# Cross-attention with its query and output weights folded into K and V, and norm chains that run on into the next stage

## The chip, the cores and the metric

One Trainium2 chip, 8 cores. Each core computes one of the eight batch elements with the same program and the same weights. The metric is the device time of the slowest core in microseconds. Some executions fall in a slow state, in which the cores of one die show a lower granted clock and the time is 3% to 16% longer; they are left out of every comparison here, for the kernel before and for every other.

Names of engines in the profile: PE is TensorE's matmuls, PEld its weight loads, DVE is VectorE, ACT ScalarE, POOL GpSimd, SP the queue that issues the large transfers. An *eviction* is the copy of a finished matmul group from PSUM into its buffer in SBUF. A line of a timeline gives start and length in us, engine, line of the kernel, operation, out<-in, shapes and count, and in brackets how long the engine stood idle before it and what ended that.

## The reference

Two layers, each FFN, token mixer, cross-attention, FFN, every part between two RMS norms. Only the attention matters here:

```python
def cross_attention(h, m, wq, wkv, wo):          # h (B, 2048, 1024), m (B, 256, 1024)
    q = (h @ wq).reshape(b, s, XA_HEADS, XA_HEAD_DIM)       # 4 heads of 256
    k, v = jnp.split(m @ wkv, 2, axis=-1)                   # 256 memory tokens
    scores = jnp.einsum("bshd,bmhd->bhsm", q, k) * (XA_HEAD_DIM ** -0.5)
    p = jax.nn.softmax(scores, axis=-1)
    o = jnp.einsum("bhsm,bmhd->bshd", p, v).reshape(b, s, D_MODEL)
    return o @ wo
# around it:
    m = rms_norm(mem, mem_norm_g[l])
    h = cross_attention(rms_norm(x, g[4]), m, xa_wq[l], xa_wkv[l], xa_wo[l])
    x = x + rms_norm(h, g[5])
```

With 256 memory tokens and heads of 256, Wq K and V Wo of a head are as large as K and V themselves, so the products may be taken in another order.

## The kernel before

Activations lie transposed, channels on the 128 partitions, the 2048 positions in four blocks of 512 ("tb"). X is the residual stream (f32), XN its normed copy (bf16), HO the output of a sub-layer before its post-norm. Weights stream from HBM as panels of 128 x 1024 into eight slots; GpSimd issues them in its own order, among its additions.

The kernel is written as a list of operations per engine, and norm work is put between matmul groups by *deferred steps*: a step has a count, every matmul group outside a step is one tick, and a step whose count has run out is emitted. A step is also forced out at once if an operation needs what it still has to write, or would overwrite what it still has to read (`_check`). The chain of a finished half (post-norm, residual add, pre-norm of the next sub-layer) is a sequence of such steps. Before the change, queueing a new sequence empties the old one on the spot:

```python
        def run_seq(steps):
            while any(d[1] == ("seq",) for d in k.deferred):
                k.need(("seq",))                 # flush of the old chain
            ...
# HalfOut.finish: the chain of two blocks ta, tb_ after the second half
                steps = [(2, fin_stats)] + [(1, A(ta, c0)) for c0 in cs]      # A: HO *= r; X += HO
                ...
                    steps += [(1, both(A(tb_, 0), sa0)), (1, A(tb_, 1)), (1, A(tb_, 2)), (1, both(A(tb_, 3), sb0)),
                              (1, A(tb_, 4)), (1, A(tb_, 5)), (1, both(A(tb_, 6), sc10)), (1, both(A(tb_, 7), sc20)),
                              (2, sa1), (3, sb1), (3, sc11), (1, sc21)]
                run_seq(steps)
```

`sa` squares four of the eight channel tiles on ScalarE, `sb_` sums them on TensorE and squares the others, `sc1` sums those, takes the reciprocal root and writes half of XN, `sc2` the rest.

Attention before, in order (cut):

```python
            for hf, c8 in [(0, c_) for c_ in range(8)]:      # Q of blocks 0, 1; memory norm among it
                w = ws.acquire(("lin", "xa_wq", l, c8))
                ...
            for hf, c8 in [(1, c_) for c_ in range(4)]: ...   # Q of blocks 2, 3, half
            for c8 in range(8): ...                           # K
            for cb in range(4): ...                           # V
            for hf, c8 in [(1, c_) for c_ in range(4, 8)]: ...
            for sb_ in range(NTB):
                for h in range(4): ...                        # scores, exp; then sum, P V, O = . / sum
            out_proj(lambda c: [("lin", "xa_wo", l, c)], rhs, 8, l, n_post, False, nxt, ho2=...)
```

The softmax here doesn't subtract the row's maximum and nothing guards it: scores larger than these inputs give would overflow.

Of the kernel before, what the change touches and what calls it, by code (L numbers as in the profile page):

```python
# [96 lines left out]
def panel_specs():  # L97
    specs = []
    for l in range(L):
        for f in range(2):  # L100
            for j in range(NJ):
                for nm, gu in (("ffn_w_gate", "g"), ("ffn_w_up", "u")):
                    specs.append((("gu", l, f, j, gu), 1024,
                                  lambda inp, c, nm=nm, l=l, f=f, j=j: _pkc(inp[nm][l, f][:, j * 128:(j + 1) * 128])))
            for c in range(8):
                for pc, (r0, r1) in enumerate(((0, 1024), (1024, 2048), (2048, 2816))):
                    specs.append((("d", l, f, c, pc), (r1 - r0),
                                  lambda inp, cc, l=l, f=f, c=c, r0=r0, r1=r1:
                                  _pkc(inp["ffn_w_down"][l, f][r0:r1, c * 128:(c + 1) * 128])))
        for nm, ncol in (("xa_wq", 8), ("xa_wkv", 8), ("xa_wo", 8)):  # L110
            for c in range(ncol):
                specs.append((("lin", nm, l, c), 1024,
                              lambda inp, cc, nm=nm, l=l, c=c: _pkc(inp[nm][l][:, c * 128:(c + 1) * 128])))
        for cb in range(4):
            for kh in range(2):
                specs.append((("wv", l, cb, kh), 1024,
                              lambda inp, cc, l=l, cb=cb, kh=kh:
                              _pkc(inp["xa_wkv"][l][kh * 512:(kh + 1) * 512, 1024 + cb * 256:1024 + (cb + 1) * 256])))
# [57 lines left out]
class K:  # L176
    ENGS = ("pe", "act", "dve", "pool", "sp")

    def __init__(self, sched=None):
# [5 lines left out]
        self._in_def = False  # L185
        self._bank = 0
# [137 lines left out]
    def _tick(self):  # L324
        if self._in_def:
            return
        for d in self.deferred:
            d[0] -= 1
# [115 lines left out]
def build(nsub=8):  # L444
# [50 lines left out]
    O = AT(nc, "O", 0, [8, S], BF16)  # L495
    HO2 = AT(nc, "HO2", 32768, [8, 1024], F32)
    Q = AT(nc, "Q", 32768, [8, S], BF16)
    M32 = AT(nc, "M32", 65536, [8, MEM], F32)
    MN = AT(nc, "MN", 73728, [8, MEM], BF16)
    KT = AT(nc, "KT", 65536, [8, MEM], BF16)  # L500
    V = AT(nc, "V", 69632, [2, D], BF16)
    ET = [AT(nc, "ET%d" % i, 86016 + i * 2048, [2, TB], BF16) for i in range(3)]
    RD = [AT(nc, "RD%d" % i, 92160 + i * 2048, [TB], F32) for i in range(2)]
# [8 lines left out]
    def program(k):  # L512
# [40 lines left out]
        def run_seq(steps):  # L553
# [9 lines left out]
            def go(i):  # L563
# [4 lines left out]
                def wrapped():  # L568
                    fn()
                    go(i + 1)  # L570
                if d <= 0:
# [64 lines left out]
        class HalfOut:  # L636
# [34 lines left out]
            def finish(self, nxt, hf, cpb=1):  # L671
# [76 lines left out]
                run_seq(steps)  # L748
# [15 lines left out]
        def out_proj(pkeys_for_c, rhs, nk, l, n_post, half, nxt, ho2=None):  # L764
            for hf in range(2):
                tbs = (2 * hf, 2 * hf + 1)
                held = []
                ho = HalfOut(l, n_post, half, tbs, hoap=(ho2 if hf == 1 else None))
# [27 lines left out]
        def ffn(l, f, n_post, nxt):  # L796
            for hf in range(2):
# [3 lines left out]
                for j in range(NJ):  # L801
                    wg = ws.acquire(("gu", l, f, j, "g"))
# [377 lines left out]

        def attention(l, n_post, nxt):
            for tb in range(NTB):
                need_xn(tb)
            m32, m32k = M32((0, 8), (0, MEM))
            k.dma("sp", lambda e: e.dma_start(out=m32, in_=memT.rearrange("(c p) m -> p c m", p=128)), "ml", writes=m32k)
            mst = {"pend": [], "mb": None, "gi": 0}

            def mem_sq(c):
                map_, mk = M32(c, (0, MEM))
                i = k.rot("SQD", 3)  # L1190
                k.op("act", lambda e: e.activation(out=SQD[i][:, 0:MEM], in_=map_, func=AF.Square),
                     reads=mk, writes=[("SQD", i)])
                mst["pend"].append((c, i))

            def mem_mm():
                c, i = mst["pend"].pop(0)
                if mst["mb"] is None:
                    mst["mb"] = k.bank(reserve=True)
                mb = mst["mb"]
                k.mm(P[mb][:, 0:MEM], [(ONESM[:, :], SQD[i][:, 0:MEM], [("SQD", i), ("ONES",)])], mb,  # L1200
                     start=(c == 0), stop=(c == 7))

            def mem_apply():
                r = rstd_from(mst["mb"], MEM, 1.0)
                for c in range(8):
                    map_, mk = M32(c, (0, MEM))
                    oap, okeys = MN(c, (0, MEM))
                    col = CF[:, CF_MG + l * 8 + c:CF_MG + l * 8 + c + 1]
                    k.op("dve", lambda e, map_=map_, oap=oap, col=col: e.scalar_tensor_tensor(
                        out=oap, in0=map_, scalar=col, in1=R[r][:, 0:MEM], op0=ALU.mult, op1=ALU.mult),  # L1210
                        reads=mk + [("R", r)] + CONST, writes=okeys)
            for hf, c8 in [(0, c_) for c_ in range(8)]:
                w = ws.acquire(("lin", "xa_wq", l, c8))
                for tb in (2 * hf, 2 * hf + 1):
                    lo, hi = tbr(tb)
                    b = k.bank()
                    k.mm(P[b][:, :], [(w.w(kk),) + tuple(_rk(XN(kk, (lo, hi)), w.key)) for kk in range(8)], b)
                    oap, okeys = Q(c8, (lo, hi))
                    evac_copy(oap, okeys, b, eng="act")
                    gi = mst["gi"]  # L1220
                    mst["gi"] += 1
                    if 6 <= gi < 14:
                        mem_mm()
                    if 4 <= gi < 12:
                        mem_sq(gi - 4)
                    if gi == 14:
                        mem_apply()
                ws.release(w)
            for hf, c8 in [(1, c_) for c_ in range(4)]:
                w = ws.acquire(("lin", "xa_wq", l, c8))  # L1230
                for tb in (2 * hf, 2 * hf + 1):
                    lo, hi = tbr(tb)
                    b = k.bank()
                    k.mm(P[b][:, :], [(w.w(kk),) + tuple(_rk(XN(kk, (lo, hi)), w.key)) for kk in range(8)], b)
                    oap, okeys = Q(c8, (lo, hi))
                    evac_copy(oap, okeys, b)
                ws.release(w)
            for c8 in range(8):
                w = ws.acquire(("lin", "xa_wkv", l, c8))
                b = k.bank()  # L1240
                k.mm(P[b][:, 0:MEM], [(w.w(kk),) + tuple(_rk(MN(kk, (0, MEM)), w.key)) for kk in range(8)], b)
                oap, okeys = KT(c8, (0, MEM))
                evac_copy(oap, okeys, b, n=MEM, eng="act")
                ws.release(w)
            for cb in range(4):
                wv0 = ws.acquire(("wv", l, cb, 0))
                wv1 = ws.acquire(("wv", l, cb, 1))
                for mt in range(2):
                    b = k.bank()
                    pairs = []  # L1250
                    for kk in range(8):
                        map_, mk = MN(kk, (mt * 128, (mt + 1) * 128))
                        sl = wv0 if kk < 4 else wv1
                        pairs.append((map_, sl.t[:, (kk % 4) * 256:(kk % 4 + 1) * 256], mk + [sl.key]))
                    k.mm(P[b][:, 0:256], pairs, b)
                    oap, okeys = V(mt, (cb * 256, (cb + 1) * 256))
                    evac_copy(oap, okeys, b, n=256)
                ws.release(wv0)
                ws.release(wv1)
            for hf, c8 in [(1, c_) for c_ in range(4, 8)]:  # L1260
                w = ws.acquire(("lin", "xa_wq", l, c8))
                for tb in (2 * hf, 2 * hf + 1):
                    lo, hi = tbr(tb)
                    b = k.bank()
                    k.mm(P[b][:, :], [(w.w(kk),) + tuple(_rk(XN(kk, (lo, hi)), w.key)) for kk in range(8)], b)
                    oap, okeys = Q(c8, (lo, hi))
                    evac_copy(oap, okeys, b)
                ws.release(w)
            for sb_ in range(NTB):
                lo, hi = tbr(sb_)  # L1270
                for h in range(4):
                    et = ET[k.rot("ET", 3)]
                    for mt in range(2):
                        b = k.bank()
                        pairs = []
                        for dc in range(2):
                            kap, kk_ = KT(2 * h + dc, (mt * 128, (mt + 1) * 128))
                            qap, qk = Q(2 * h + dc, (lo, hi))
                            pairs.append((kap, qap, kk_ + qk))
                        k.mm(P[b][:, :], pairs, b)  # L1280
                        eap, ek = et(mt, (0, TB))
                        k.op("act", lambda e, b=b, eap=eap: e.activation(out=eap, in_=P[b][:, :], func=AF.Exp, scale=1.0 / 16.0),  # L1282
# [120 lines left out]
```

## Time and profile before

| | before |
|---|---|
| time, fast runs | 2968.9 to 2972.2 us, median 2970.4 |
| matmuls (weight loads) | 12574 |
| TensorE busy, VectorE, ScalarE, GpSimd | 93%, 35%, 33%, 21% |
| one attention, mixer end to FFN start | 280 us (layer 0), 276 us (layer 1) |
| of that lost by TensorE | 62 and 61 us |

A matmul's record lasts 0.38 us, though dense 512-column matmuls start every 0.216 us; so busy time overlaps and hides lost time. The weight loads, one per matmul, times the dense pace give the time that a stretch would need; the rest of the stretch is lost, to waits or to the half clock. The lines are shown in the prediction, whose "Trace Analysis" is the Trainium skill's page "Perfetto Trace Analysis".

### The profile page before, as it was taken

The numbers are of one execution on the slowest core, as the hardware profiler recorded it, in microseconds if no ns is written. First come the engines' busy times: TensorE is split into PE (matmuls) and PEld (weight loads), VectorE is DVE, ScalarE is ACT, GpSimd is POOL, SyncE is SP. The second block draws the span as 40 slices with busy tenths as digits, with TensorE's granted clock in tenths as the row PEclk, the third lists the DMA queues.
The fourth block names the chain that finished last, engine by engine and source line by source line (L and its number), as shares of the span: only waits on it lengthen the run. The fifth ranks groups of instructions, "written<-read, shape, count | busy, mean of one in ns | idle before, by whom it ended". The sixth has DMA issues, their size and how long they took to land.

```text
span 2968.9 us, 36707 instructions; the slowest of 8 cores (2963.8 to 2968.9 us)
## 1 busy us (share of the span) xinstructions
PE 2748.3 (93%) x12329; PEld 1231.4 (41%) x12574; DVE 1028.5 (35%) x1362; ACT 990.6 (33%) x1481; POOL 627.0 (21%) x915
## 2 busy tenths in 40 slices
PE   6999999976889899999999999979997898999996
PEld 2444444432334344444444444433443443444443
DVE  3211410774453451051052042135537236213212
ACT  4213312434636631241241242121146365113112
POOL 1113311221230221141121141120013113111121
PEclk9999999987999999999999999988999998999998
DMA  7554554523343345455455445431143523545567
GB/s 171 75 72 74 78 69 83 79 44 57 64 68 58 47 71 77 69 79 75 69 79 76 71 77 76 73 51 29 33 72 54 86 36 58 78 71 107 104 93 145
DMA packets 125510, 218.55 MB, mean 74 GB/s; under 512 B 14352, under 2 KB 29968, under 8 KB 125328
## 3 DMA queue, kind: packets, MB, share of 16 engines
q0 software_dynamic: 108432, 192.70, 43.6%
q1 hardware_dynamic: 16896, 23.48, 2.6%
q8 instruction: 107, 1.75, 0.2%
q14 instruction: 75, 0.61, 0.1%
HBM read 396.19 MB, written 8.39 MB: 136 GB/s over the span
## 4 chain that ended last, share of the span: by engine, by line
PE 82%; DVE 8%; ACT 5%; issue 3%; DMA 2%; POOL 0%; DVEq 0%; ACTq 0%; POOLq 0%; SPq 0%
PE ps L288 82%; DVE HO L695 3%; DVE XN L606 1%; DMA slot<-wflat 1%; DVE X L697 1%; ACT sqp L600 1%; ACT RD L1294 0%; ACT ET L1282 0%; DVE FE L919 0%; ACT r L538 0%; ACT RD L1295 0%; DVE ET L919 0%; DMA X<-xT 0%; ACT sqp L593 0%; ACT L538 0%
## 5 line engine op out<-in xcount | busy, mean ns | idle before, releaser
L288 PE MATMUL ps<-XN,slot 128*128 128x512 bf16 x7152 | 1621.7, 384 | 64.4 <-DVE XN L606 39.3
L288 PEld LDWEIGHTS ps<-XN,slot 128*128 128x128 bf16 x7296 | 718.6, 99 | 957.5 <-issue 123.6
L389 POOL DMA_DIRECT2D slot<-wflat x752 | 399.6, 536 | 2107.5 <-PE ps L288 2053.7
L823 DVE TENSOR_TENSOR H<-ps,s 128x512 bf16<-128x512 f32 x352 | 241.6, 689 | 1116.2 <-PE ps L288 1091.5
L288 PE MATMUL ps<-H,slot 128*128 128x512 bf16 x2756 | 622.4, 379 | 4.2 <-DMA slot<-wflat 1.1
L814 ACT ACTIVATE s<-ps 128x512 f32<-128x512 f32 x352 | 209.0, 597 | 801.8 <-PE ps L288 731.9
L288 PEld LDWEIGHTS ps<-H,slot 128*128 128x128 bf16 x2816 | 275.2, 98 | 334.6 <-issue 3.5
L652 ACT ACTIVATE HO<-ps,cf_sb 128x512 f32<-128x512 f32 x256 | 176.0, 688 | 535.5 <-PE ps L288 512.8
L695 DVE TENSOR_TENSOR HO<-HO,r 128x512 f32<-128x512 f32 x192 | 201.7, 1078 | 262.1 <-ACT r L540 262.1
L606 DVE SCALAR_TENSOR_TENSOR XN<-X,cf_sb,r 128x512 bf16<-128x512 f32 x256 | 176.7, 758 | 142.5 <-ACT r L540 142.5
L697 POOL TENSOR_TENSOR X<-X,HO 128x512 f32<-128x512 f32 x104 | 154.9, 1516 | 102.9 <-DVE HO L695 93.1
L655 ACT ACTIVATE sqd<-ps 128x512 bf16<-128x512 f32 x256 | 152.1, 594 | 58.7 <-PE ps L288 58.7
L288 PE MATMUL ps<-sqp,onesm 128*128 128x512 bf16 x251 | 78.6, 442 | 61.6 <-ACT sqp L593 33.8
L288 PE MATMUL ps<-O,slot 128*128 128x512 bf16 x500 | 117.7, 379 | 0.8
L288 PE MATMUL ps<-sqd,onesm 128*128 128x512 bf16 (+1 forms) x269 | 97.4, 378 | 13.1 <-ACT sqd L655 12.7
L733 DVE TENSOR_TENSOR HO<-HO,r 128x512 f32<-128x512 f32 x64 | 44.7, 732 | 140.0 <-ACT r L540 140.0
L600 ACT ACTIVATE sqp<-X 128x2048 bf16<-128x2048 f32 x32 | 61.1, 1909 | 62.8 <-PE ps L288 42.7
L288 PEld LDWEIGHTS ps<-O,slot 128*128 128x128 bf16 x512 | 49.9, 98 | 60.7 <-issue 1.1
L697 DVE TENSOR_TENSOR X<-X,HO 128x512 f32<-128x512 f32 x88 | 65.3, 742 | 9.5 <-DVE HO L695 0.5
L288 PEld LDWEIGHTS ps<-sqp,onesm 128*128 128x128 bf16 x256 | 25.6, 106 | 101.2 <-issue 81.3
L1141 ACT ACTIVATE s<-ps 128x512 f32<-128x512 f32 x32 | 19.1, 596 | 141.0 <-PE ps L288 115.0
L593 ACT ACTIVATE sqp<-X 128x2048 bf16<-128x2048 f32 x32 | 60.9, 1904 | 12.2 <-POOL X L697 12.2
(100 smaller groups left out, 1245.5 us busy)
## 6 DMA issues: line engine op xcount, KB each, us to landing
slot<-wflat POOLq DMA_DIRECT2D x680, 256.0 KB, 4.7
slot<-wflat POOLq DMA_DIRECT2D x72, 192.0 KB, 4.3
X<-xT SPq DMA_DIRECT2D x8, 1024.0 KB, 25.3
yT<-X SPq DMA_DIRECT2D x4, 2048.0 KB, 12.1
CP<-CR SPq DMA_DIRECT2D x64, 32.0 KB, 2.8
YB<-YP SPq DMA_DIRECT2D x64, 32.0 KB, 1.8
M<-memT SPq DMA_DIRECT2D x2, 1024.0 KB, 13.1
WT<-wt SPq DMA_DIRECT2D x1, 288.0 KB, 5.0
```

Of the source, the lines that this page charges most:

```text
L288: fn = (lambda e, l_=l_, r_=r_, st=st, sp=sp: e.matmul(out, lhsT=l_, rhs=r_, start=st, stop=sp))
L389: self.k.dma("pool", lambda e, dst=dst, src=src: e.dma_start(out=dst, in_=src), "w%d" % idx, reads=([("X", c, 0) for c in range(4)] if i = ...
L593: k.op("act", lambda e: e.activation(out=SQP[:, :, :], in_=X[:, 0:4, lo:hi], func=AF.Square), reads=[xk(c, tb) for c in range(4)], writes= ...
L600: k.op("act", lambda e: e.activation(out=SQP[:, :, :], in_=X[:, 4:8, lo:hi], func=AF.Square), reads=[xk(c, tb) for c in range(4, 8)], writ ...
L606: k.op("dve", lambda e, c=c, oap=oap: e.scalar_tensor_tensor(out=oap, in0=X[:, c, lo:hi], scalar=G(l, n, c), in1=R[r][:, :], op0=ALU.mult, ...
L652: k.op("act", lambda e: e.activation(out=oap, in_=P[bank][:, :], func=AF.Copy, scale=gcol), reads=[("P", bank)] + CONST, writes=okeys)
L655: k.op("act", lambda e: e.activation(out=SQD[i][:, :], in_=P[bank][:, :], func=AF.Square), reads=[("P", bank)], writes=[("SQD", i)])
L695: k.op("dve", lambda e, hap=hap: e.tensor_tensor(out=hap, in0=hap, in1=R[r][:, :], op=ALU.mult), reads=hkeys + [("R", r)], writes=hkeys)
L697: k.op(add_eng_for(tb), lambda e, hap=hap, c=c: e.tensor_tensor(out=X[:, c, lo:hi], in0=X[:, c, lo:hi], in1=hap, op=ALU.add), reads=hkeys ...
L733: k.op("dve", lambda e, hap=hap, r=r: e.tensor_tensor(out=hap, in0=hap, in1=R[r][:, :], op=ALU.mult), reads=hkeys + [("R", r)], writes=hkeys)
L814: k.op("act", lambda e, bg=bg, s=s: e.activation(out=SS[s][:, :], in_=P[bg][:, :], func=AF.Silu), reads=[("P", bg)], writes=[("S", s)])
L823: k.op("dve", lambda e, bu=bu, s=s, hap=hap: e.tensor_tensor(out=hap, in0=P[bu][:, :], in1=SS[s][:, :], op=ALU.mult), reads=[("P", bu), (" ...
```

## The change

Its intent: fewer matmul columns (neither Q nor O is formed), no flush of the norm chains at the two hand-overs of attention, and the memory norm once instead of per layer.

```diff
+        def run_seq(steps, lazy=False):
+            if lazy:                              # append to what is left of the old chain
+                idx = [i for i, d in enumerate(k.deferred) if d[1] == ("seq",)]
+                if idx:
+                    d = k.deferred.pop(idx[0])
+                    old = SEQ["rest"]
+                    steps = [(max(d[0], 0.001), old[0][1])] + list(old[1:]) + list(steps)
             while any(d[1] == ("seq",) for d in k.deferred):
                 k.need(("seq",))
...
-                run_seq(steps)
+                run_seq(steps, lazy=(hf == 1 and not self.half and nxt is not None))
+            def finish1(self, nxt):               # chain of one block; adds on GpSimd
+                run_seq([(2, fin_stats), (1, A(0)), ..., (1, A(7)), (2, sa), (2, sb_), (3, sc1), (1, sc2)], lazy=True)
...
+    WQK = AT(nc, "WQK", 32768, [8, 1024], BF16)
+    HA = AT(nc, "HA", 77824, [8, TB], F32)
+    VWO = AT(nc, "VWO", 94208, [8, D], BF16)      # HO is 77824 .. 110592
...
+                    if l == 0 and f == 0 and hf == 0 and j == 10:
+                        mem_norm()                # both layers; kept in HBM, loaded at the mixer's end
...
+            for h in range(2):                    # attention, in order
+                proj_t(KT, 2 * h, 2 * h)
+                proj_t(KT, 2 * h + 1, 2 * h + 1)
+            for h in range(2):
+                wqk(h)
+            for h in range(4):
+                if h < 2:
+                    proj_t(KT, 2 * h + 4, 2 * h + 4)
+                    proj_t(KT, 2 * h + 5, 2 * h + 5)
+                scores(0, h)
+                if h < 2:
+                    wqk(h + 2)
+            for h in range(4):
+                proj_t(VT, 8 + 2 * h, 2 * h)
+                proj_t(VT, 9 + 2 * h, 2 * h + 1)
+                scores(1, h)
+                vwo(h)
+            out(0)
+            for tb in range(2, NTB):
+                for h in range(4):
+                    scores(tb, h)
+                out(tb - 1)
+            out(NTB - 1)
```

`proj_t` is eight matmuls of 256 columns and one eviction, for K always on ScalarE, for V alternating between ScalarE and VectorE (`eng=("act" if pc < 8 else None)`). `wqk(h)` and `vwo(h)` make the folded weights of a head, `scores(tb, h)` takes XN times them, and `out(tb)` is the whole output of one block. A group shorter than eight 512-column matmuls now counts as a part of a tick (`tickw`: 0.5 for a group of K or V, 0.25 in `vwo`, 0.125 in `wqk`).

## The prediction

> **What bounds the kernel now.** I read the page first: TensorE is busy nearly everywhere and everything else a third of the time, so the kernel is a stream of matmuls with holes. Then I cut each attention, with the end of the mixer's output projection before it and the start of the FFN after it, into stretches, and compared the time of each with what its weight loads (one per matmul, recorded without losses, unlike the matmuls) would take at full pace.
>
> ```profile
> PE 2748.3 (93%) x12329; PEld 1231.4 (41%) x12574; DVE 1028.5 (35%) x1362; ACT 990.6 (33%) x1481; POOL 627.0 (21%) x915
> PE   6999999976889899999999999979997898999996
> ```
>
> The 93% hides the holes: slices 10 to 14 (layer 0's mixer end and attention) and 30 to 33 (layer 1's) fall to 7 or 8. The stretches of layer 0's attention, and one line for the whole of layer 1's:
>
> ```profile
> core 4: us, PE busy (x) PEld busy (x) DVE busy (x) ACT busy (x) POOL busy (x), PEclk, DMA share, GB/s
> 792.60:873.10 80.50, 60.78 (x236) 24.12 (x239) 51.60 (x68) 38.14 (x56) 19.28 (x22) 0.87 0.42 68
> 873.10:895.80 22.70, 15.30 (x129) 11.95 (x129) 1.70 (x4) 4.82 (x12) 7.91 (x15) 1.00 0.94 136
> 895.80:947.30 51.50, 48.88 (x214) 20.20 (x218) 21.23 (x33) 35.34 (x64) 3.17 (x6) 1.00 0.33 50
> 947.30:1011.80 64.50, 63.60 (x289) 28.56 (x293) 24.98 (x28) 38.70 (x67) 20.02 (x24) 1.00 0.30 43
> 1011.80:1026.60 14.80, 5.83 (x15) 1.67 (x16) 5.39 (x8) 10.76 (x13) 0.00 (x0) 0.61 0.63 100
> 1026.60:1072.80 46.20, 41.22 (x183) 17.99 (x186) 39.52 (x50) 27.06 (x29) 17.13 (x18) 0.98 0.37 56
> ...
> 2239.60:2516.00 276.40, 237.72 (x1049) 105.51 (x1067) 142.47 (x188) 152.28 (x238) 67.15 (x84) 0.93 0.40 60
> ```
>
> Layer 0's six stretches are 280.2 us with 1078 loads, 136 of them for 256 columns (64 K, 64 V, 8 memory statistics). Pace: in the dense output projection eight 512-column matmuls start 1.72 to 1.73 us apart, 0.216 us each; the 64 K matmuls span 7.15 us with a last one of 0.27, so 0.109 each. Ideal: 942 x 0.216 + 136 x 0.109 = 203 + 15 = 218 us. **Lost: 62 us.** Layer 1: 931 x 0.216 + 15 = 216 of 276.4, **lost 61 us.** By stretch, same sum: about 29 in the first (mixer end and first Q blocks), 8 in K and V, 4 in scores, 1 in the output projection, 12 in the hand-over to the FFN, 6 in the FFN's start. What these holes are, from the timelines of TensorE and GpSimd:
>
> ```profile
> 797.29 1.91 PE L288 MATMUL ps<-sqp,onesm 128*128 128x512 bf16 x4 [3.17 <-ACT sqd L655]
> 803.62 1.86 PE L288 MATMUL ps<-sqp,onesm 128*128 128x512 bf16 x4 [4.00 <-ACT sqp L593]
> 807.64 1.87 PE L288 MATMUL ps<-sqp,onesm 128*128 128x512 bf16 x4 [2.15 <-ACT sqp L600]
> ...
> 855.63 17.63 PE L288 MATMUL ps<-XN,slot 128*128 128x512 bf16 x55 [4.88 <-DVE XN L606]
> ...
> 890.94 1.95 PE L288 MATMUL ps<-slot,MN 128*128 128x256 bf16 x16 [1.32 <-DMA slot<-wflat]
> 894.30 1.47 PE L288 MATMUL ps<-slot,MN 128*128 128x256 bf16 x12 [1.40 <-DMA slot<-wflat]
> ...
> 1020.90 1.86 PE L288 MATMUL ps<-sqp,onesm 128*128 128x512 bf16 x4 [4.05 <-ACT sqp L593]
> 1024.91 1.87 PE L288 MATMUL ps<-sqp,onesm 128*128 128x512 bf16 x4 [2.15 <-ACT sqp L600]
> ...
> 790.54 3.36 POOL L389 DMA_DIRECT2D slot<-wflat  x6
> ```
>
> The reader is to see three things. The pre-norm chain (square, statistics, reciprocal root, XN) of the first half is flushed, one step waiting for the last, when the second half's chain is queued: 4.00 and 2.15, and 4.05 and 2.15 at the FFN. Four statistics matmuls take 1.9 us there against 1.03 in a dense stretch: the clock is halved (the windows grant 0.61). And V waits for weight panels, though nothing else is loaded then.
>
> **What the Trainium skill says.** "TensorE: Matmul & The Clock Gate", section "What's actually happening": idle windows of about 3.4 us halve the clock, about 3.4 us of sustained work restores it. The trace agrees: after the 4.88 us hole, one-microsecond windows grant 0.50 from 855 to 864 and 1.00 from 865, which turns 5 us of idleness into about 10 lost. Same page, "Back-to-back issue gap": N/2.4 + 2.5 ns for warm isolated matmuls, which is 215.8 and 109.2 ns; the trace shows just these, and not the 131 ns it gives as the sustained figure. "Trace Analysis", section "Identifying the Most-Contended Engine": matmul busy share is no measure of headroom, loads are better; hence the counting of loads. "DMA: Bandwidth & Descriptors", section "Measured (HBM→SBUF, 128 partitions, SWDGE, issued from GpSimd)", gives 341 GB/s for 1 MB. Here a 256 KB bf16 panel is read as 512 KB of f32; with the queue full the trace moves 142 to 170 GB/s at the bf16 side, so one panel per 1.6 to 1.8 us, twice that in HBM bytes, near the page's value. I use the trace's.
>
> **The change part by part.** It folds Wq into K (scores = XN x (Wq K)) and Wo into V, so that neither Q nor O exists, and it lets a chain of norm steps run on into the next stage.
>
> 1. *Matmuls, per layer.* Removed: Q 256, scores 64, PV 64, Wo 256 of 512 columns = 640. Added: scores directly from XN 256, output from probabilities 256, V-Wo product 32 = 544. K and V stay at 64 + 64 of 256 columns; the Wq-K product adds 64. So 96 x 0.216 = 20.7 less, 64 x 0.109 = 7.0 more: **13.7 us per layer, 27.4 in all.** The memory norm is done once, so its statistics cost 8 instead of 16 matmuls: 0.9. Sum **28.3 us**, all on the path, since TensorE is the bound.
>
> 2. *Flush at mixer to attention.* Attention now starts with K and Wq-K, which need no XN, and the old steps run by ticks among them. One tick is about 1.73 us of TensorE. At the end of the projection the first half's chain has some 7 ticks left, the first scores come at tick 5 with block 0 already normed, block 1 is wanted at tick 17, blocks 2 and 3 at tick 46 and beyond while the second half's 27 steps end near tick 34. So the 4.00, 2.15, the small XN waits of 0.29 and the hole of 4.88 go, with their cold clock. What remains is the 3.17 us wait for the held evictions, which is in the mixer, and a cold start after it (half of 3.4 to 7 us): **about 6 of the 29 us stay.**
>
> 3. *Weight panels.* Before: 48 a layer (Wq twice, Wo twice). Now 32, but each used only 0.87 us, all within the first 55 us. Four panels with one scores block take 6.9 us, that is 1.73 per panel, against 1.6 to 1.8 that the DMA gives: just balanced. At the start six panels were issued only at 790.54, behind GpSimd's residual adds, and land by about 803; K and Wq-K at half clock reach the last of them at about the same time. Estimate **2 us instead of 8**.
>
> 4. *Attention's evictions.* The 0.16 us bubbles before the softmax sums go, because 16 matmuls instead of 4 lie between. VectorE gets HO (1.08 us each), residual adds and XN (0.76 each) at one per tick; two bursts of eight XN, some 5 us, stand in front of the evictions of V and V-Wo. **About 3 instead of 5 us.**
>
> 5. *Flush at attention to FFN.* Four one-block chains of 18 ticks; the first three fit within the remaining scores and outputs, the last runs in the FFN's first half, which needs blocks 0 and 1 only. The 12 us go; in the FFN's start one block is to be normed, not four: **2 instead of 18 us.**
>
> Left per layer: 6 + 2 + 3 + 2 = 13 us, against 62 and 61; saved 49 + 48 = 97.
>
> 6. *Memory norm in the first FFN:* 16 VectorE operations of 0.48 us (7.7 us) queue ahead of the gated products; eight PSUM banks hold about four tiles of 3.45 us, so I count 1 us. Its trip through HBM lands long before use.
>
> Sum: 28.3 + 97 - 1 = 124 us. From 2970 (the fast runs are 2969.2, 2970.4 and 2971.2; 3083 and 3109 are slow) to **2846 us.**
>
> **The rivals.** *DMA takes the place of the chain.* For it: 32 panels in 55 us need 1.73 us each, the queue's full rate, and GpSimd also makes 8 adds of 1.5 us per block in the same order as the issues. Against it: traffic falls by a third, and the 7 us of scores(0, heads 2 and 3) let the queue catch up. If the supply is 2.2 us per panel, 32 x 0.45 = 14 us more per layer: about 2875. *VectorE or ScalarE becomes the bound.* For it: the stall of 2.38 us behind HO in the FFN, and the single queue, in which an eviction waits behind a norm. Against it: in the stretches above each is busy for half the time. It would cost 5 to 10 us per layer: 2855 to 2866. *Only arithmetic counts,* the holes moving elsewhere as the same norms still have to be done: 2942, within 2%. Against it: the flush is a serial wait and not work. *Denser TensorE lowers its clock.* Long dense FFN windows are granted 1.00, so I see no sign of it.
>
> **Range and chances.** No hole left at all: 2970 - 28 - 123 = 2819. Half of them left: 2970 - 28 - 61 + 1 = 2882. So 2822 to 2885 for 8 in 10. The limit for 2% is 2911, which needs two thirds of the holes to stay: faster 0.95, same 0.04, slower 0.01.
>
> **What would show it.** Loads fall by only 72 in the whole kernel: 192 fewer of 512 columns, 120 more of 256; no flush waits of 4 us for the squares at the four hand-overs; the granted clock near 1.00 through attention but for some microseconds at its start; few waits for weight panels. I am wrong if panel waits or VectorE evictions in the K and V phase exceed 10 us per layer, or if the clock stays halved there.

## The result and the profile after

Nine runs of the changed kernel, eight of them fast: 2861.4 to 2862.8 us, median 2861.9; before, twelve fast of fifteen, median 2970.4. The ratio is 0.9636 (95%: 0.9626 to 0.9645), and a second time, on another chip, 0.9639. Ratios here are the mean time of one kernel's fast runs over that of the other's of the same rounds, so not quite the ratio of the medians. Executions in which one die ran at a lower clock are left out of the means. That is 108.5 us or 3.6% less; predicted were 124 us and 2846, with a range of 2822 to 2885. So the direction, the size and the range held, and 16 us of the gain are missing.

The page of the changed kernel, engines and the slices of TensorE:

```profile
PE 2687.3 (94%) x12254; PEld 1225.1 (43%) x12502; DVE 1010.9 (35%) x1330; ACT 981.2 (34%) x1462; POOL 657.0 (23%) x915
PE   6999999986989999999999999997999899999996
```

12502 loads are 72 fewer, as counted. Before, slices 11, 12 and 14 and again 31, 32 and 34, where the two attentions and their hand-overs lie, were at seven or eight; now one eight is left in each group, in slices 12 and 32. The same kind of stretches as before, layer 0 (columns: stretch, its length, then busy time and count of each engine, granted clock, share of the DMA engines, GB/s):

```profile
795.73:802.50 6.77, 3.61 (x13) 1.38 (x12) 0.00 (x0) 5.19 (x8) 1.15 (x3) 0.79 0.95 123
802.50:814.70 12.20, 10.15 (x84) 8.17 (x84) 5.39 (x8) 11.12 (x19) 4.32 (x9) 0.97 1.03 161
814.70:841.80 27.10, 26.94 (x157) 15.36 (x158) 17.41 (x23) 16.71 (x33) 13.88 (x15) 1.00 0.74 112
841.80:878.70 36.90, 29.46 (x149) 15.21 (x151) 27.95 (x44) 22.80 (x34) 9.07 (x16) 0.95 0.59 93
878.70:979.80 101.10, 97.31 (x444) 44.08 (x452) 58.59 (x68) 70.21 (x114) 35.46 (x25) 1.00 0.05 9
979.80:1026.00 46.20, 45.59 (x209) 20.51 (x211) 26.06 (x33) 26.30 (x30) 19.61 (x22) 1.00 0.41 60
```

With 0.216 us per load of 512 columns and 0.109 per load of 256 (79 of the 84 in the second line, 64 of the 158 in the third, 48 of the 151 in the fourth), the stretches lose 4.2, 2.5, 0, **9.4**, 3.5 and 0.6 us: 20.2, where 62 were lost before and 13 were predicted. Layer 1 by the same sum: 19.3. What was predicted, and what came:

| part | predicted | measured |
|---|---|---|
| matmuls | 72 fewer loads, 28.3 us | 72 fewer loads |
| left at the mixer's end, per layer | 6 | 4.2 + 2.5 = 6.7 |
| left to weight panels | 2 | no such wait in either attention |
| left in the V and V-Wo phase and scores | 3 | 9.4 (layer 0), 8.7 (layer 1) |
| left at the hand-over to the FFN and in its start | 2 | 3.5 + 0.6 = 4.1 (layer 1: 3.8) |
| memory norm in the first FFN, with its matmuls | 1 + 0.9 | 2.8 |

The last row comes from one point of the first FFN's down projection: the same statistics matmul starts at 256.26 in the old trace and at 259.10 in the new one. Of the missing 16 us, 13.5 are in the two attentions (20.2 + 19.3 - 26) and 1 here. The account closes: 28.3 of arithmetic, plus 62 + 61 - 39.5 of holes, less 1.9 for the waits of the memory norm, is 110 us, against 108.5 measured.

The flush is gone. TensorE's timeline, the hand-overs and the V phase:

```profile
800.41 1.91 PE L288 MATMUL ps<-sqp,onesm 128*128 128x512 bf16 x4 [3.16 <-ACT sqd L668]
802.12 0.63 PE L288 MATMUL ps<-sqd,onesm 128*128 128x512 bf16 x1
802.54 3.95 PE L288 MATMUL ps<-MN,slot 128*128 128x256 bf16 x32
807.60 1.92 PE L288 MATMUL ps<-KT,slot 128*128 128x256 bf16 x16 [1.11 <-ACT KT L794]
...
813.03 1.91 PE L288 MATMUL ps<-MN,slot 128*128 128x256 bf16 x16 [0.89 <-ACT WQK L1276]
...
857.03 2.06 PE L288 MATMUL ps<-slot,VT 128*128 128x512 bf16 x6 [3.22 <-ACT ET L1310]
...
867.76 1.89 PE L288 MATMUL ps<-slot,VT 128*128 128x512 bf16 x8 [1.53 <-DVE VT L797]
...
919.37 1.02 PE L288 MATMUL ps<-sqp,onesm 128*128 128x512 bf16 x4 [1.66 <-ACT sqp L606]
...
979.90 3.62 PE L288 MATMUL ps<-XN,slot 128*128 128x512 bf16 x16
```

K starts directly behind the mixer's last statistics instead of after 4.00, 2.15 and the XN waits, and the FFN starts without a hole. Two short waits for ScalarE's evictions of K and of the folded weights, 1.11 and 0.89 us, are new. Weight panels hold nobody up in attention; TensorE's waits for them in the whole kernel, before and then after:

```profile
PE ps L288 <- DMA slot<-wflat: 12.8, 14, 1.4
```
```profile
PE ps L288 <- DMA slot<-wflat: 2.9, 4, 1.2
```

What is new is a hole of 3.22 us in the V phase, with the clock halved soon after it (granted 0.50 from 858 to 861; the sixteen V matmuls at 859.74 take 2.61 us instead of 1.91), and some of 1.2 to 1.5 us for V evictions and an exponential. The hole is put down to ScalarE's exponential, but ScalarE itself stood still. Its timeline there:

```profile
847.83 1.89 ACT L613 ACTIVATE sqp<-X 128x2048 bf16<-128x2048 f32 x1
854.25 0.60 ACT L794 ACTIVATE VWO<-ps 128x512 bf16<-128x512 f32 x1 [4.53 <-DVE X L710]
854.74 0.38 ACT L794 ACTIVATE VT<-ps 128x256 bf16<-128x256 f32 x1
```

An eviction into VWO waits for a residual step of VectorE. VWO lies on HO's second half: row 0 of VWO is HO of channel tile 4, block 2; row 1 is the same tile, block 3. The first two rows are wanted when block 3's residual steps have only just begun.

### The profile page after: what moved, and what is told of

It reads as the page before. It is cut to its first block, busy times and chain, and to the rows that moved or that the text cites. A ratio compares the mean times of both kernels' runs of the same rounds, so it can differ in the third digit from the quotient of the medians.

```text
span 2860.0 us, 36293 instructions; the slowest of 8 cores (2854.2 to 2860.0 us)
## 1 busy us (share of the span) xinstructions
PE 2687.3 (94%) x12254; PEld 1225.1 (43%) x12502; DVE 1010.9 (35%) x1330; ACT 981.2 (34%) x1462; POOL 657.0 (23%) x915
## 4 chain that ended last, share of the span: by engine, by line
PE 89%; DVE 4%; ACT 3%; issue 3%; DMA 1%; POOL 0%; DVEq 0%; ACTq 0%; SPq 0%; POOLq 0%
PE ps L288 89%; DVE XN L619 1%; DVE HO L708 1%; DVE FE L958 0%; DMA slot<-wflat 0%; ACT sqp L613 0%; ACT sqp L606 0%; DVE ET L958 0%; DVE X L710 0%; DMA X<-xT 0%; DVE YF L1065 0%; ACT sqd L668 0%; ACT L541 0%; DVE MNL L1236 0%; POOL X L710 0%
## 5 line engine op out<-in xcount | busy, mean ns | idle before, releaser
L288 PE MATMUL ps<-XN,slot 128*128 128x512 bf16 x6651 | 1491.3, 382 | 43.2 <-DVE XN L619 22.1
L288 PEld LDWEIGHTS ps<-XN,slot 128*128 128x128 bf16 x6784 | 666.7, 98 | 860.8 <-issue 75.4
L708 DVE TENSOR_TENSOR HO<-HO,r 128x512 f32<-128x512 f32 x160 | 159.7, 1022 | 255.5 <-ACT r L543 255.2
L288 PE MATMUL ps<-ET,VWO 128*128 128x512 bf16 x502 | 118.8, 379 | 0.6
L288 PE MATMUL ps<-XN,WQK 128*128 128x512 bf16 x502 | 116.2, 379 | 0.5
L778 POOL TENSOR_TENSOR X<-X,HA 128x512 f32<-128x512 f32 x48 | 72.5, 1532 | 129.9 <-ACT ET L1310 69.5
L288 PE MATMUL ps<-sqd,onesm 128*128 128x512 bf16 x246 | 89.9, 382 | 6.4 <-ACT sqd L668 6.2
L613 ACT ACTIVATE sqp<-X 128x2048 bf16<-128x2048 f32 x32 | 61.1, 1909 | 50.0 <-PE ps L288 33.9
L1328 DVE TENSOR_TENSOR ET<-ET,s 128x512 bf16<-128x512 bf16 x64 | 62.9, 1023 | 39.3 <-ACT s L1324 39.3
L288 PEld LDWEIGHTS ps<-ET,VWO 128*128 128x128 bf16 x512 | 50.1, 98 | 60.5
```

The lines of the kernel that those rows point to most:

```text
L288: fn = (lambda e, l_=l_, r_=r_, st=st, sp=sp: e.matmul(out, lhsT=l_, rhs=r_, start=st, stop=sp))
L613: k.op("act", lambda e: e.activation(out=SQP[:, :, :], in_=X[:, 4:8, lo:hi], func=AF.Square), reads=[xk(c, tb) for c in range(4, 8)], writ ...
L708: k.op("dve", lambda e, hap=hap: e.tensor_tensor(out=hap, in0=hap, in1=R[r][:, :], op=ALU.mult), reads=hkeys + [("R", r)], writes=hkeys)
L778: k.op("pool", lambda e: e.tensor_tensor(out=X[:, c, lo:hi], in0=X[:, c, lo:hi], in1=hap, op=ALU.add), reads=hkeys + [xk(c, tb)], writes=[ ...
L1328: k.op("dve", lambda e, eap=eap: e.tensor_tensor(out=eap, in0=eap, in1=SS[s][:, :], op=ALU.mult), reads=ek + [("S", s)], writes=ek)
```

## The experiments

All outputs are right. "Base" is the changed kernel at 2861.9 (2861.2 on the chip of the second group). The kernel before was run beside each group, with fast medians of 2971.1, 2968.9 and 2969.2, so groups differ by less than 0.1%. The third group (e11 to e14) has no run of the base beside it, and e11 and e14 have only two fast runs of six each. Times are medians of fast runs.

| run | ratio to before | us | against the base |
|---|---|---|---|
| e4_nofold | 0.9838 | 2922.6 | +61 |
| e2_mixflush | 0.9696 | 2880.4 | +18 |
| e3_attflush | 0.9700 | 2880.9 | +19 |
| e1_rows | 0.9674 | 2873.6 | +12 |
| e14_vtdve | 0.9675 | 2873.0 | +11 |
| e8_rows_pool | 0.9664 | 2869.2 | +8 |
| e11_vtact | 0.9657 | 2867.5 | +6 |
| after_again | 0.9639 | 2861.2 | the base |
| e7_rows_vtact | 0.9602 | 2850.7 | -11 |
| e9_rows_vtact_pool | 0.9602 | 2850.8 | -10 |
| e12_rows_vtact_sb | 0.9586 | 2846.1 | -16 |
| e13_rows_vtact_sb_mem | 0.9602 | 2846.9 | -15 |

**Was the gain in the holes or in the arithmetic?** The kernel before, with its own products, in the order of the changed one (the edit in words where it is long):

```diff
-                run_seq(steps)
+                run_seq(steps, lazy=(hf == 1 and not self.half and self.mix))   # mixers only
+  mem_norm() in the first FFN, mem_load(l) at the mixer's end, as in the changed kernel
-  attention: Q(0,1), half of Q(2,3), K, V, rest of Q(2,3), scores
+  attention: K, Q(0,1), V, scores of blocks 0 and 1, Q(2,3), scores of blocks 2 and 3
   out_proj(...) unchanged, with its flush before the FFN
```

> The kernel before with its own products (Q, K, V, O, Wo) but the changed kernel's order at the start: memory norm once in the first FFN, K first, the mixer's norm chain running on, scores of blocks 0 and 1 before Q of blocks 2 and 3. The output projection and its flush before the FFN stay. Theory A (most of the gain is in the holes, only 28 us in the arithmetic): from the 62 us lost per layer about 29 + 3 go except for some 8 that stay and some 4 more for V's panels, so 20 us per layer: about 2930 us (2920 to 2940). Theory B (only the folded arithmetic counts): 2965 us or more.

Measured 2922.6, within theory A's range. With no product folded, the order, the running-on and the memory norm done once give 48 us of the 108. "Only the arithmetic counts" falls. The other 61 us are the folding, 28 by count, together with the one-block outputs, which this kernel can't have as it stands. How those 33 divide was not taken apart further. The panel waits that I feared here did not come; small waits for O and V did.

**The flush at the mixer's end.**

```diff
-                run_seq(steps, lazy=(hf == 1 and not self.half and nxt is not None))
+                run_seq(steps)
```

> The changed kernel, but at the end of a mixer the old norm chain is flushed when the new one is queued, as before. Theory A (serial flush is what the holes at the mixer's end were): the waits of about 4.0 and 2.1 us for the squares come back and K starts some 7 us later, 6 to 9 us per layer: 2874 to 2880 us. Theory B (the gain is the fewer matmuls and the one-block output, not the running-on of the chain): within 3 us of 2862.

Measured 2880.4, just above theory A's range. The waits are back in TensorE's timeline, digit for digit as in the kernel before, and K starts at 811 after them:

```profile
805.52 1.86 PE L288 MATMUL ps<-sqp,onesm 128*128 128x512 bf16 x4 [4.00 <-ACT sqp L606]
809.53 1.87 PE L288 MATMUL ps<-sqp,onesm 128*128 128x512 bf16 x4 [2.15 <-ACT sqp L613]
811.19 5.78 PE L288 MATMUL ps<-MN,slot 128*128 128x256 bf16 x32
```

**The flush between the one-block outputs.**

```diff
-                         (1, A(7)), (2, sa), (2, sb_), (3, sc1), (1, sc2)], lazy=True)
+                         (1, A(7)), (2, sa), (2, sb_), (3, sc1), (1, sc2)])
```

> The changed kernel, but each one-block chain of the attention's output flushes the one before it. Theory A (the chains of 18 ticks nearly fit between the outputs by themselves, so it is the cut into four one-block outputs that removed the flush before the FFN, not the running-on): 2860 to 2866 us. Theory B (running-on is needed there too): 8 us or more per layer, 2878 us or more.

My theory A fell: 2880.9. I had counted that the chain of block 2 needs 18 ticks and the last output gives 14 to 16, and took the two steps left over for free. They are not:

```profile
985.09 1.87 PE L288 MATMUL ps<-sqp,onesm 128*128 128x512 bf16 x4 [3.85 <-ACT sqp L613]
986.75 5.37 PE L288 MATMUL ps<-XN,slot 128*128 128x512 bf16 x16
```

One forced step is a wait of 3.85 us for the square behind it, and then a low clock: four statistics matmuls take 1.87 us instead of 1.03 and the first 16 of the FFN 5.37 instead of 3.62. So the running-on is needed at the FFN too, not only the cut into one-block outputs.

**The hole of the V phase, first theory.** Let VWO's rows lie so that the first two heads' rows cover HO of block 2, whose steps come first:

```diff
+            def vrow(j):
+                return 2 * j if j < 4 else 2 * (j - 4) + 1
-                        oap, okeys = VWO(2 * h + mt, ...)        # and VWO(j, ...) in out()
+                        oap, okeys = VWO(vrow(2 * h + mt), ...)
```

> The changed kernel with only the order of VWO's rows permuted, so that the first two heads' rows fall on the half of the HO buffer whose residual steps come first. Theory A (the V-Wo evictions wait, write after read, for HO rows that the last residual steps still have to read, and ScalarE, which waits there, keeps the exponentials behind it): the waits of TensorE for ET of about 3.2 and 1.2 us and the half clock after them go, 5 to 7 us per layer, so 2848 to 2852 us. Theory B (VectorE and ScalarE are just too busy in that phase): no change, 2860 to 2863 us.

Neither theory had this: 12 us **slower**. ScalarE no longer stands still, but TensorE's timeline has a longer hole, at another place, and VectorE's shows what it waited for:

```profile
867.82 3.57 PE L288 MATMUL ps<-slot,VT 128*128 128x512 bf16 x8 [5.01 <-DVE VT L797]
871.19 3.04 PE L288 MATMUL ps<-MN,slot 128*128 128x256 bf16 x16
```
```profile
863.10 0.69 DVE L708 TENSOR_TENSOR HO<-HO,r 128x512 f32<-128x512 f32 x1
863.89 0.69 DVE L710 TENSOR_TENSOR X<-X,HO 128x512 f32<-128x512 f32 x1
864.50 2.73 DVE L619 SCALAR_TENSOR_TENSOR XN<-X,cf_sb,r 128x512 bf16<-128x512 f32 x4
867.15 0.42 DVE L797 CAST VT<-ps 128x256 bf16<-128x256 f32 x1
```

The V eviction takes 0.42 us, but it stands at the end of VectorE's queue of residual steps and XN. Next in TensorE's program stands `vwo(h)`, which needs all of V's rows of the head, so TensorE waits. After this hole of 5.01 us the clock is halved too: the eight matmuls after it take 3.57 us instead of 1.89. This suggests two causes in a row, where taking away the first lets TensorE run into the second at a worse place; the next kernels test it.

The three altered kernels of the first group came out slower than I had expected of them (e3 lay within its theory B).

> The changed kernel once more, unaltered, as the base for the runs beside it: the three runs with one part undone or altered came out at 2875 to 2882 us, above all expectations, with cores that differ by up to 13 us. Theory A (the altered order costs that): 2861 to 2864 us as before. Theory B (this kernel's short holes make a cold clock on some chips and cores and not on others): 2865 us or more here, with cores further apart than the 6 us of before.

2861.2: theory A, the base is stable; the slower times are the kernels' own.

**The second cause taken away as well:** V evictions on ScalarE alone.

```diff
-                evac_copy(oap, okeys, b, n=MEM, eng=("act" if pc < 8 else None))
+                evac_copy(oap, okeys, b, n=MEM, eng="act")        # e7: with the rows; e11: without
```

> The permuted rows of VWO, and the evictions of V all on ScalarE, none on VectorE. Theory A (in the V phase VectorE's queue of residual steps, XN and softmax products is the bound, and a V eviction at its end holds TensorE): the waits for VT, 14 us in the kernel with the permuted rows alone, go with the cold clock after them: 8 to 16 us less than that kernel (2875), so 2859 to 2867 us, and less than the unaltered one by 3 to 8 us. Theory B (ScalarE has no room either, the waits move to it): as the kernel with permuted rows, 2870 us or more.

2850.7: 23 us below the permuted rows alone, more than expected, and 10.5 below the base. Theory A holds. In the same 41 us, from 841 to 882, the base (first fence), the permuted rows (second) and this kernel (third) got this done; the second count in brackets is weight loads, the last number but two the granted clock:

```profile
841.00:882.00 41.00, 33.56 (x169) 17.08 (x171) 32.05 (x50) 25.42 (x39) 10.93 (x18) 0.96 0.60 93
```
```profile
841.00:882.00 41.00, 32.69 (x160) 16.11 (x158) 29.34 (x46) 23.70 (x35) 10.65 (x18) 0.92 0.64 90
```
```profile
841.00:882.00 41.00, 38.02 (x198) 18.83 (x197) 33.89 (x51) 31.02 (x50) 11.28 (x18) 1.00 0.67 103
```

**Is the first cause real?** The V evictions on ScalarE without the permuted rows.

> The changed kernel with its own VWO rows, but all V evictions on ScalarE. Theory A (two causes in a row: ScalarE stands still until the last HO rows under VWO are read, and V evictions behind VectorE's queue; taking the second away alone leaves the first, now with the V evictions behind it): 2858 to 2866 us, little or nothing gained. Theory B (only the V evictions on VectorE matter, the rows did nothing but harm): 2848 to 2853 us, as with rows and V on ScalarE (2851).

2867.5, just above the range of theory A and far from B: alone this change gains nothing; it is 6 us slower, from two fast runs on another chip than the base's. ScalarE still stops for 4.09 us, now with the V evictions behind it, and TensorE later stops for VectorE's V-Wo eviction. ScalarE's line, then TensorE's:

```profile
852.35 0.60 ACT L794 ACTIVATE VWO<-ps 128x512 bf16<-128x512 f32 x1 [4.09 <-DVE X L710]
```
```profile
863.29 3.44 PE L288 MATMUL ps<-XN,WQK 128*128 128x512 bf16 x8 [3.44 <-DVE VWO L797]
```

With the base, the rows, the V evictions and both, this makes a square of four: 2861, 2874, 2868 and 2851. Neither helps alone, both together do. The wait for HO is write-after-read: the old content of the memory has to be read before VWO may overwrite it. Placing the rows only moves it to rows that are read earlier. A kernel in which VWO has memory of its own was not run: by the kernel's memory map XN, WQK, both ET, KT, VT, MN and HO fill the 110592 bytes of the working area at that time, and VWO needs 16 KB.

**The suspected cost doubled:** all V evictions on VectorE, own rows (`eng=("act" if pc < 8 else "dve")`).

> The changed kernel with all V evictions on VectorE, the suspected cost doubled. If VectorE's queue holds them: later by 3 to 8 us per layer, 2868 to 2878 us. If the queue did not matter: 2860 to 2864 us.

2873.0, as the queue theory said.

**VectorE relieved of additions instead.**

```diff
-                    return "pool" if tb == ta else "dve"
+                    return "pool" if (tb == ta or not self.half) else "dve"   # e8: with rows; e9: with rows and V on ScalarE
```

> The permuted rows of VWO, and the residual adds of the last block of a mixer on GpSimd instead of VectorE (8 of 0.69 us per layer). Theory A (VectorE's work is the bound): V evictions come 5 us earlier, 4 to 8 us per layer: 2860 to 2867 us. Theory B (VectorE's products take 1.7 us instead of 0.69 while GpSimd adds, as the trace shows for the first block, so the queue gets no shorter): 2872 to 2880 us, as with the rows alone.

2869.2: 4 us better than the rows alone, between the two ranges, 2 us above A's and 3 below B's. Taking eight additions off VectorE gains little; what the traces show for it is that VectorE's own products are slower while GpSimd adds. From VectorE's timeline of the base, the same product of block 2, with GpSimd at work, and of block 3, without:

```profile
841.09 1.70 DVE L708 TENSOR_TENSOR HO<-HO,r 128x512 f32<-128x512 f32 x1
...
846.67 0.69 DVE L708 TENSOR_TENSOR HO<-HO,r 128x512 f32<-128x512 f32 x1
```

And in this kernel, beside the moved additions, four XN products that took 2.73 us with the rows alone:

```profile
853.85 3.96 DVE L619 SCALAR_TENSOR_TENSOR XN<-X,cf_sb,r 128x512 bf16<-128x512 f32 x4 [0.73 <-ACT r L543]
```

> All three: permuted rows, V evictions on ScalarE, last block's adds on GpSimd. If the V evictions behind VectorE's queue were the whole hole, this is within 3 us of the kernel with rows and V evictions on ScalarE; if VectorE's queue also holds the V-Wo evictions or the XN, 4 us or more below it.

2850.8, the same as without it: with V on ScalarE, VectorE's additions no longer matter. The hole is not gone altogether: by the loads, 9.2 of the base's 41 us above are lost and 3.6 in the kernel with rows and V on ScalarE, one wait of 1.65 us for an exponential among them. The difference, 5.6 us per layer, accounts for the 10.5 us.

**The two waits of 1.66 us per layer** in the output, for the square of the pre-norm, and the memory norm.

```diff
-                         (1, A(7)), (2, sa), (2, sb_), (3, sc1), (1, sc2)], lazy=True)
+                         (1, A(7)), (2, sa), (4, sb_), (3, sc1), (1, sc2)], lazy=True)
-            k.defer(4, ("mem",), m_apply, ...                # e13 only
+            k.defer(7, ("mem",), m_apply, ...
```

> Permuted rows, V evictions on ScalarE, and four ticks instead of two between the first square of a block's pre-norm and its statistics matmuls. If the two waits of 1.66 us for the square in each layer's output are due to that spacing, they go: 2851 less 6.6 is 2844 us. If the square is late for another reason, they move with it: 2851 us.

2846.1: 4.6 of the hoped 6.6 us. The waits for the square in the output are gone; one behind ScalarE's reciprocal root has come in their place, in the FFN's start:

```profile
986.47 3.83 PE L288 MATMUL ps<-XN,slot 128*128 128x512 bf16 x17 [1.60 <-ACT r L541]
```

This is the fastest kernel, 0.9586 of the kernel before.

> The same, and the memory norm's statistics 7 instead of 4 ticks after its square. The hoisted norm cost 2.8 us in the first FFN, 0.9 of it the matmuls, 1.0 a wait for the square and 0.8 a wait behind VectorE; this takes the 1.0 away: 1 us below the run beside it, so 2843 us.

No gain, and it could not have one: the two kernels turned out to be the same program on every engine, but for the order of two semaphore waits. The statistics step stands in the queue behind the square's step, which waits 14 ticks; a count of 4 or of 7 has long run out by then, and the statistics follow the square at once either way. The wait in the first FFN is the same, here in this kernel:

```profile
139.85 1.03 PE L288 MATMUL ps<-MSQ,onesm 128*128 128x256 bf16 x8 [1.02 <-ACT MSQ L1226]
```

It serves as a repetition: 2846.9, though one of its six runs, 2874.2, lifts the ratio to 0.9602.

## Why the prediction was right or wrong

It was right in what carries it: that the kernel is a stream of matmuls with 62 lost microseconds in each attention, that most of them are waits of the norm chains plus the half clock after them, and that the gain is the 28 us of arithmetic plus most of the holes. Step by step:

- *Step 1, matmuls.* The count of loads came out exactly, 72 fewer.
- *Step 2, mixer to attention.* "About 6 of the 29 us stay": 6.7. This is luck in part: 2.0 of the 6.7 are the waits for ScalarE's evictions of K and WQK, which I did not have, and the cold start cost less than I had allowed for. Putting the flush back costs 18 us for two layers, so the flush is shown to be the cause of 18 of the 45 us saved here. The rest, the small XN waits and the hole of 4.88 us, goes with K coming first; the kernel without folding shows that only together with the running-on.
- *Step 3, weight panels.* Estimated 2 us, measured none, which hides 4 us of the other misses. The rival in which DMA becomes the bound fell: the panels arrived in time although the queue ran at its full rate in the first 12 us.
- *Step 4, attention's evictions.* This is the term that was wrong. "About 3 instead of 5 us" was 9.4 and 8.7, close to the 10 us per layer that I had named as a sign of being wrong; the granted clock of this stretch was 0.95. I had the length of VectorE's queue about right, but not what depends on it: a V eviction at its end holds `vwo`, and thereby TensorE, and VWO's first rows cover HO rows that are read last, which stops ScalarE with the exponentials behind it. Both could be read from the code, one from the two buffers' addresses, the other from the alternating engine of V's evictions. My rival "VectorE or ScalarE becomes the bound", 2855 to 2866 us, is where the time came out. The eviction behind VectorE's queue is what that rival named; the wait of VWO's rows for HO was in none of my rivals. The four kernels of the square show that it took both.
- *Step 5, attention to FFN.* "2 instead of 18": 4.1 and 3.8. Most of it is two waits of 1.66 us, for a square only two ticks ahead of its statistics. The running-on is worth 19 us in all there, as its removal shows; in the experiment's expectation I had called it needless.
- *Step 6, memory norm.* 1.9 with its matmuls, measured 2.8: I had missed the wait of 1.0 us for the square of 128 x 2048.

Redone from the lines it shows, the prediction's split of the 62 us is 29.7, 8.5, 4.4, 1.2, 11.3 and 6.0: its "12 in the hand-over" is 11. (The loads of the six lines add to 1081 and not 1078, as one that crosses an edge counts on both sides.)

The sum of the misses: 20.2 + 19.3 - 26 = 13.5 and 1 for the memory norm, of the 16 that were missing. The repairs to step 4 and step 5, in the fastest kernel, bring back 16 us. That this ends on the estimate itself, 2846, is partly chance, as step 3 came out 2 us per layer better; the two that I did not repair, the mixer's held evictions (3.16 us in the timeline) and the memory norm, were in it from the start or are small.

## What to carry to other kernels

When a deferred chain is no longer flushed, it runs on beside the next stage; check then which of that stage's evictions stand behind it in the same engine's queue, and which of its buffers lie on memory the chain has still to read. A hole with two causes in a row can get longer when only one of them is taken away, so try the pair before giving up either. Count loads against the dense pace to find how much is lost, since busy time shows 93% where 123 us are lost in two attentions.

## What the Trainium skill lacked or had wrong

- "TensorE: Matmul & The Clock Gate", section "Back-to-back issue gap", gives 131 ns as the sustained spacing of 512-column matmuls; in every dense stretch here it is 216 ns, the page's own isolated figure (which it also gives, in other sections, for matmuls back to back).
- The same page, section "What's actually happening", sets idle windows of about 3.4 us for the half clock. Here a hole of 2.78 us, at the mixer's end of layer 1, already leads to it: half-microsecond windows grant 0.94 at 2188.5 and 0.50 from 2189.0, before work goes on at 2189.37, and four statistics matmuls take 1.91 us against 1.03 when dense. (The same place in layer 0 shows 3.16 us, but its first matmul's record seems to be missing: its weight load stands at 800.00.) The ten slow microseconds after the hole of 4.88 us in the kernel before do not speak against the page: until the full clock came at 864.6, the matmuls were dense only from 860.5 on.
- "GPSIMD Engine Reference", section "1. Specifications", says that GpSimd shares its SBUF interfaces with VectorE and that operations with two SBUF inputs contend; I found no figure for a VectorE product against a GpSimd addition. Here a VectorE product of 128 x 512 f32 takes 1.70 us while GpSimd adds and 0.69 us otherwise.
- No page that I read warns that with statically placed buffers a write-after-read wait stops an in-order engine together with unrelated work behind it; here 4.53 us of ScalarE, with the exponentials behind it.
